# Five token groups instead of six in the input projection and the gates of a hybrid attention layer

## The chip, the cores and the metric

The kernel runs on one core of a Trainium2 chip. The metric is the device time of one execution in microseconds. The kernel before was timed three times: the median is 2660.56 us, the runs lie between 2659.95 and 2668.45 us.

## What is computed

One layer of a streaming encoder on 2176 tokens: 2048 of a new stream and 128 (8 streams of 16) that continue running streams with 2048 cached positions each. The model width is 1024. All arithmetic is float32. Cut to what matters:

```python
h    = rms_norm(x, g_in)
proj = einsum('btd,de->bte', h, w_in)
qa, ka, va, z_a, qd, ckv_in, kpe_in, z_b, m_a, m_b = split(proj)   # 512,512,512,512,512,256,64,512,1024,1024 columns
o_a  = diff_attention(rope(qa), rope(ka), va)       # 4 heads, chunk-causal mask
o_b  = mla_attention(q_lat, q_pe, ckv_rows, kpe_rows)  # 4 heads, chunk-causal mask
y_a  = (rms_norm(o_a, g_sub) * silu(z_a)) @ w_oa
y_b  = (o_b @ w_uv * silu(z_b)) @ w_ob
out  = x + (sigmoid(m_a) * y_a + sigmoid(m_b) * y_b) @ w_out
y    = rms_norm(out, g_final)
```

The rotated keys, the values, the compressed rows and the rotated positional keys are outputs too.

## The kernel before, in words

Float32 products are made of three passes: each operand is split into a high part in the type float32r and a low part (the rest), and the products high*high, low*high and high*low are added in PSUM (`_mm3`, lines 95 to 101). A product over the model width has eight row tiles of 128, so it is 24 matmuls, each with a new 128x128 weight and a moving tile as wide as the token group.

**Groups.** `GROUPS` (line 38) cuts the 2176 tokens into five groups of 384 and one of 256. All stages but the attention go by these groups.

**Phase A** (`_phase_a`, lines 127 to 347) is the input projection. `load_group` (151) loads a group of the transposed input in four staging tiles of two row tiles, writes the high and low parts `hi` and `lo` (they stay on chip until the phase ends) and sums the squares in a tile `sq`. `first_units` (271) does this while two units of 128 output columns are projected group by group; `stats` (184) makes the norm from the squares. A unit is one `unit_psum` per group (24 matmuls into one PSUM bank), and blocks of two units follow: `units`, `rope_block`, `kpe_block`, `v_block`. There are 14 units through `units` and `first_units` and 8 through the rope blocks; the key block has 16 matmuls per group, and the value blocks go by 128 tokens and don't depend on the groups. Each block's weights come through `weights` (201): a staging tile (`stage`, 141: of three one comes from the pool `a_s` with one buffer, the others from the outer pool `z_s` with two), a split on ACT and DVE, and a pair of buffers out of three pairs (`z_w` four buffers, `a_w` two). After blocks 2 to 9 the split weights of two gate units each are written to a scratch tensor `wz` (lines 342 to 347).

**Gates** (`_gates`, 350 to 389) are 16 more units of the same projection, done later as work that fills TensorE: the tile scheduler orders all instructions ahead of time by priority and by a model of their times, the gates' loads and splits have the priority of the end of phase A, their matmuls that of the code's place behind phase B. One group's `z_hi` and `z_lo` are on chip at a time (pool `z_h`, one buffer). Each unit has one PSUM bank (pool `z_p`, one buffer), which ACT empties with a tanh into a tile of `z_t` (4 buffers) that is stored to `smT`. Groups 0, 1, 3 and 4 load and split the weights anew, groups 2 and 5 load the split ones (`ready`). Groups 0, 1, 2 and 5 stand ahead of the sample part, 3 and 4 are tied behind the last attention matmul (lines 1276 to 1280).

**Phase A2** (`_phase_a2`) makes the latent queries, keys and values by groups. **Phase B** (`_phase_b`) is the attention of the 2048 tokens, four heads of each kind side by side: in eight steps the differential head goes up through the query blocks and the latent head goes down, so that at each step both together need 20 key and value tiles of 128x512. These tiles come from the pool `c_kv` with 25 buffers (line 925), loaded in the order of the code at line 943 and given to any buffer that has come free. At a change of heads 16 tiles of the new latent head and 4 of the new differential head take the place of the old ones. **The sample part** (`_sample`) reads the caches, and **phase C** (`_phase_c`) is the output side, by groups again. All DMAs of these parts are issued on SP's queue, in the order of the schedule.

Of the kernel before, what the change touches and what calls it, by code (L numbers as in the profile page):

```python
# [20 lines left out]
P = 128  # L21
# [15 lines left out]
NG = 384  # L37
GROUPS = [(t, min(NG, T - t)) for t in range(0, T, NG)]

# [76 lines left out]
def _outer(c, stack):  # L116

    tc = c.tc

    def pool(name, bufs, **kw):  # L120
        return stack.enter_context(tc.tile_pool(name=name, bufs=bufs, **kw))

    c.zh, c.zw, c.zs, c.zt = pool("z_h", 1), pool("z_w", 4), pool("z_s", 2), pool("z_t", 4)
    c.zp = pool("z_p", 1, space=PSUM)


def _phase_a(c):
    nc, tc = c.nc, c.tc
    with (
        tc.tile_pool(name="a_h", bufs=1) as ph,  # L130
        tc.tile_pool(name="a_w", bufs=2) as pw,
        tc.tile_pool(name="a_s", bufs=1) as pst,
        tc.tile_pool(name="a_t", bufs=6) as pt,
# [5 lines left out]
        count = {"st": 0, "w": 0, "t": 0}  # L139
# [11 lines left out]
        def load_group(g):  # L151
# [6 lines left out]
            for k2 in range(4):  # L158
# [62 lines left out]
        def rope_block(u0, dst, pair, out, scale):  # L221
            ws = [weights(c.i["wu"][u0 + i], f"u{u0 + i}") for i in range(2)]
            for g, (t0, n) in enumerate(GROUPS):
# [7 lines left out]
                ta, tb = tmp(n, f"ta{nm}"), tmp(n, f"tb{nm}")  # L231
# [160 lines left out]
def _phase_a2(c):  # L392
    nc, tc = c.nc, c.tc
    with (
# [20 lines left out]
        def tmp(n, name, m=P):  # L415
            return pt.tile([P, NG], F32, tag="t", name=name)[:m, :n]
# [11 lines left out]
        def prep(g):  # L428
            t0, n = GROUPS[g]
            qd = pn.tile([P, 4, NG], F32, tag="qd", name=f"qd{g}", bufs=1)[:, :, :n]  # L430
            nc.sync.dma_start(qd, c.qdT[:, :, t0 : t0 + n].rearrange("k p n -> p k n"))
            ck = pn.tile([P, 2, NG], F32, tag="ck", name=f"ck{g}", bufs=1)[:, :, :n]
            nc.sync.dma_start(ck, c.ckT[:, :, t0 : t0 + n].rearrange("k p n -> p k n"))
            sq = pn.tile([P, 4, NG], F32, tag="sq", name=f"sq{g}", bufs=1)[:, :, :n]
# [3 lines left out]
            sk = pn.tile([P, 2, NG], F32, tag="sk", name=f"sk{g}", bufs=1)[:, :, :n]  # L438
# [17 lines left out]
            for j, r in enumerate(rs):  # L456
# [5 lines left out]
                R = pn.tile([P, NG], F32, tag=f"R{j}", name=f"R{g}_{j}", bufs=1)[:, :n]  # L462
                nc.scalar.copy(R, pr[:, :n])
                Rs.append(R)
            qh = pn.tile([P, 4, NG], F32R, tag="qh", name=f"qh{g}")[:, :, :n]
            ql = pn.tile([P, 4, NG], F32R, tag="ql", name=f"ql{g}")[:, :, :n]
# [5 lines left out]
            ch = pn.tile([P, 2, NG], F32R, tag="ch", name=f"ch{g}")[:, :, :n]  # L472
            cl = pn.tile([P, 2, NG], F32R, tag="cl", name=f"cl{g}")[:, :, :n]
# [17 lines left out]
        def kpe(g):  # L491
            t0, n = GROUPS[g]
            cols = slice(t0, t0 + n)
            parts = pn.tile([64, 2, 2, NG], F32, tag="kp", name=f"kp{g}", bufs=1)[:, :, :, :n]
# [881 lines left out]
```

## Time and profile before

| | before |
|---|---|
| median of 3 runs | 2660.56 us |
| the profiled execution's own time | 2664.33 us |
| its span (first to last instruction) | 2662.4 us |
| mean granted TensorE clock | 0.975 |
| PE busy | 2521.9 us, 95% of the span |
| DVE / ACT / POOL busy | 54% / 40% / 26% |
| HBM traffic | 185 GB/s over the span |

A busy PE is read with care: the records of matmuls overlap, so that one of 334 ns can follow another after 173 ns. What a matmul costs in a steady stream is the distance of the starts. The granted clock stands as a share of 2.4 GHz; 0.50 is 1.2 GHz.

### The profile page before, as it was taken

What the parts mean: (1) busy time and instruction counts of PE and PEld (TensorE: products, weight loads), DVE (VectorE), ACT (ScalarE), POOL (GpSimd) and SP (SyncE); (2) the same over time, 40 slices, a digit from 0 to 9 for tenths busy, and PEclk for the clock granted to TensorE, in tenths of its full rate; (3) what the DMA queues carried; (4) which work ended last, traced back from release to release, by engine and by line L of the source; (5) the groups of instructions that cost most, each with busy time, mean ns of one, the idle gap of its engine ahead of it and who ended that gap; (6) DMA issues with size and microseconds to landing.
All of it is one profiled execution on the core that took longest, in us unless ns stands there. A gap on an engine that the chain in (4) does not pass through costs nothing. (4 is left out here: it accounts for less than half of the span.)

```text
span 2662.4 us, 44907 instructions
## 1 busy us (share of the span) xinstructions
PE 2521.9 (95%) x16308; PEld 2257.0 (85%) x16308; DVE 1438.3 (54%) x3038; ACT 1066.4 (40%) x2682; POOL 705.4 (26%) x946
## 2 busy tenths in 40 slices
PE   7999999999888989999999999998999998999998
PEld 7999999999787879998988898887676775888887
DVE  8236762233565657877785577896323323533334
ACT  5111213212334356766674566775334333311111
POOL 7102220001343433334343333544101001112212
PEclk9999999999898999999999999999999998999999
DMA  5345777422567893365566658523887676533332
GB/s 182 113 156 200 252 255 228 150 69 82 165 226 242 263 281 108 123 184 155 172 184 185 206 173 246 152 76 119 343 334 293 253 308 225 182 126 119 124 101 101
DMA packets 291372, 496.17 MB, mean 186 GB/s; under 512 B 27440, under 2 KB 229200, under 8 KB 280144
## 3 DMA queue, kind: packets, MB, share of 16 engines
q1 hardware_dynamic: 291152, 493.31, 55.9%
q8 instruction: 129, 2.11, 0.3%
q14 instruction: 91, 0.75, 0.1%
HBM read 351.55 MB, written 141.66 MB: 185 GB/s over the span
## 5 line engine op out<-in xcount | busy, mean ns | idle before, releaser
L98 PE MATMUL z<-z_hi,zw 128*128 128x384 f32 (+1 forms) x768 | 261.8, 341 | 21.9 <-ACT zt L388 18.5
L99 PE MATMUL z<-z_lo,zw 128*128 128x384 f32 (+1 forms) x768 | 257.1, 335 | 0.6 <-POOL z_lo L370 0.6
L100 PE MATMUL z<-z_hi,zw 128*128 128x384 f32 (+1 forms) x768 | 256.3, 334 | 0.4 <-DVE zw L113 0.2
L990 DVE TENSOR_REDUCE pmd<-sd 128x1 f32<-128x512 f32 (+3 forms) x320 | 189.3, 602 | 56.6 <-PE sd L1091 28.0
L992 ACT ACTIVATE ed<-sd,pmd 128x512 f32<-128x512 f32 (+3 forms) x320 | 200.7, 632 | 47.8 <-DVE pmd L990 32.2
L1091 PE MATMUL sd<-k,q 128*128 128x512 f32 (+2 forms) x640 | 190.2, 384 | 5.0 <-ACT ed L992 2.7
L1031 POOL TENSOR_SCALAR ed<-ed,ad 128x512 f32<-128x512 f32 (+3 forms) x160 | 115.6, 739 | 279.7 <-DVE ad L1007 129.4
L98 PEld LDWEIGHTS z<-z_hi,zw 128*128 128x128 f32 x768 | 147.2, 192 | 41.1 <-ACT zt L388 24.4
L99 PEld LDWEIGHTS z<-z_lo,zw 128*128 128x128 f32 x768 | 146.9, 191 | 8.9 <-issue 6.3
L100 PEld LDWEIGHTS z<-z_hi,zw 128*128 128x128 f32 x768 | 146.7, 191 | 6.7 <-issue 3.7
L1031 POOL TENSOR_SCALAR em<-em,am 128x512 f32<-128x512 f32 (+3 forms) x160 | 104.5, 669 | 154.3 <-DVE am L1007 108.9
L98 PE MATMUL y<-o,wh_ab 128*128 128x384 f32 (+1 forms) x384 | 129.5, 337 | 14.2 <-DVE sm L1210 12.5
L370 POOL TENSOR_TENSOR z_lo<-zx,z_hi 128x384 fp32r<-128x384 f32 (+1 forms) x48 | 48.5, 1038 | 329.6 <-DVE gt L260 261.6
L113 DVE TENSOR_TENSOR zw<-zs,zw 128x512 fp32r<-128x512 f32 x128 | 89.6, 727 | 82.4 <-ACT zw L112 82.1
L98 PE MATMUL ps_u<-hi,wh_u 128*128 128x384 f32 (+1 forms) x384 | 126.0, 328 | 6.1 <-ACT wh_u L112 6.1
L99 PE MATMUL y<-o,wh_ab 128*128 128x384 f32 (+1 forms) x384 | 128.0, 333 | 0.4 <-DVE o L113 0.4
L1215 ACT ACTIVATE m<-sm 128x384 fp32r<-128x384 f32 (+1 forms) x48 | 24.4, 507 | 258.6 <-POOL sm L1213 258.6
L100 PE MATMUL y<-o,wl_ab 128*128 128x384 f32 (+1 forms) x384 | 127.8, 333 | 0.0
L98 PE MATMUL ps_z<-hi,wh_z 128*128 128x384 f32 (+1 forms) x384 | 125.1, 326 | 1.0 <-ACT wh_z L112 1.0
L99 PE MATMUL ps_u<-lo,wh_u 128*128 128x384 f32 (+1 forms) x384 | 125.6, 327 | 0.0
L100 PE MATMUL ps_u<-hi,wl_u 128*128 128x384 f32 (+1 forms) x384 | 125.0, 327 | 0.0
L99 PE MATMUL ps_z<-lo,wh_z 128*128 128x384 f32 (+1 forms) x384 | 125.0, 325 | 0.0
(364 smaller groups left out, 7539.1 us busy)
## 6 DMA issues: line engine op xcount, KB each, us to landing
zs<-in_wu_dram SPq DMA_DIRECT2D x64, 512.0 KB
zw<-wz SPq DMA_DIRECT2D x64, 512.0 KB
ksd<-in_ckT_dram SPq DMA_DIRECT2D x32, 1024.0 KB
vsd<-in_cv_dram SPq DMA_DIRECT2D x32, 1024.0 KB
q<-Qs SPq DMA_DIRECT2D x128, 128.0 KB
ksm<-in_cc_dram SPq DMA_DIRECT2D x16, 1024.0 KB
smT<-zt SPq DMA_DIRECT2D x80, 192.0 KB
sm<-smT SPq DMA_DIRECT2D x80, 192.0 KB
```

What stands on the lines that cost most here:

```text
L98: nc.tensor.matmul(out, ah, bh, start=(j == 0), stop=False)
L99: nc.tensor.matmul(out, ah, bl, start=False, stop=False)
L100: last = nc.tensor.matmul(out, al, bh, start=False, stop=(j == n - 1))
L113: nc.vector.tensor_tensor(lo, src, hi.bitcast(F32), op=ALU.subtract)
L370: nc.gpsimd.tensor_tensor(lo[:, k], x[:, j], hi[:, k].bitcast(F32), op=ALU.subtract)
L990: nc.vector.tensor_reduce(nm_, ps[:, :w], axis=AX.X, op=ALU.max, negate=True)
L992: nc.scalar.activation(e[:, :w], ps[:, :w], AF.Exp, bias=nm_, accum_out=l[:, s, i : i + 1])
L1031: nc.gpsimd.tensor_scalar(p, p, a[:, 0, j : j + 1], 1.0, op0=ALU.mult, op1=ALU.mult)
L1091: nc.tensor.matmul(ps[:, :n], qs[s][:, j, qc], ks[s].tiles[i][:, :n], start=(j == 0), stop=(j == 1 and not last))
L1215: nc.scalar.mul(z[0], sm[0], 0.5)
```

## The change

Phase A and the gates go by five groups, two of 512 and three of 384 tokens (`GROUPS`); phases A2 and C keep the six old ones under the name `CGROUPS`. As the tiles of 512 need more room, other buffers go: the pool `a_s` (third staging buffer of phase A), one of four buffers of `z_t`, one of six of `a_t`, and four of 25 key and value buffers of `c_kv`. The sums of squares and two temporaries of the rope blocks move from `a_c` and `a_t` into `z_t` (`tmp2`). The gates are done for groups 0, 1 and 2 ahead of the sample part (before: 0, 1, 2 and 5), only group 2 with weights that are split already.

```diff
-NG = 384
-GROUPS = [(t, min(NG, T - t)) for t in range(0, T, NG)]
+NG = 512
+GROUPS = [(0, 512), (512, 512), (1024, 384), (1408, 384), (1792, 384)]
+NC = 384
+CGROUPS = [(t, min(NC, T - t)) for t in range(0, T, NC)]
...
-    c.zh, c.zw, c.zs, c.zt = pool("z_h", 1), pool("z_w", 4), pool("z_s", 2), pool("z_t", 4)
+    c.zh, c.zw, c.zs, c.zt = pool("z_h", 1), pool("z_w", 4), pool("z_s", 2), pool("z_t", 3)
...
-        tc.tile_pool(name="a_s", bufs=1) as pst,
-        tc.tile_pool(name="a_t", bufs=6) as pt,
+        tc.tile_pool(name="a_t", bufs=5) as pt,
...
         def stage(shape, name):
-            count["st"] += 1
-            return (pst if count["st"] % 3 == 0 else c.zs).tile(shape, F32, tag="st", name=name)
+            return c.zs.tile(shape, F32, tag="st", name=name)
...
-                        total = pc.tile([P, NG], F32, tag="sq", name=f"sq{g}", bufs=2)[:, :n]
+                        total = tmp2(n, f"sq{g}")
...
-                ta, tb = tmp(n, f"ta{nm}"), tmp(n, f"tb{nm}")
+                ta, tb = tmp2(n, f"ta{nm}"), tmp2(n, f"tb{nm}")
...
-        tc.tile_pool(name="c_kv", bufs=25, reuse_waits="tile") as pkv,
+        tc.tile_pool(name="c_kv", bufs=21, reuse_waits="tile") as pkv,
...
-            for g in (0, 1, 2, 5):
-                _gates(c, prio, g, None, g in (2, 5))
+            for g in (0, 1, 2):
+                _gates(c, prio, g, None, g == 2)
```

The lines left out put `CGROUPS` and `NC` for `GROUPS` and `NG` in phases A2 and C and change nothing else there.

## Rows read from the trace of the kernel before

**Rows 1.** The page, busy time of PE: engine, us, share, instructions.

```profile
PE 2521.9 (95%) x16308; PEld 2257.0 (85%) x16308; DVE 1438.3 (54%) x3038; ACT 1066.4 (40%) x2682; POOL 705.4 (26%) x946
```

**Rows 2.** Windows: us, busy us of PE, PEld, DVE, ACT, POOL; PEclk, DMA share, GB/s.

```profile
0.00:70.00 70.00, 53.39 (x268) 51.07 (x269) 59.47 (x87) 38.14 (x75) 51.83 (x65) 0.93 0.58 185
70.00:655.00 585.00, 572.24 (x3675) 571.16 (x3674) 245.42 (x394) 116.42 (x204) 63.47 (x60) 0.99 0.50 166
...
690.00:938.00 248.00, 208.88 (x1119) 198.16 (x1118) 150.70 (x242) 97.27 (x191) 100.24 (x94) 0.90 0.76 240
...
1391.00:1641.00 250.00, 240.70 (x1628) 215.62 (x1627) 165.24 (x425) 144.78 (x416) 87.25 (x137) 0.98 0.65 202
1641.00:1850.00 209.00, 197.10 (x1305) 168.37 (x1305) 170.30 (x447) 143.69 (x415) 93.78 (x142) 0.98 0.38 112
```

**Rows 3.** PE's timeline, width 384, first and last of 97: start us, us.

```profile
99.80 0.33 PE L99 MATMUL ps_qd<-lo,wh_qd 128*128 128x384 f32 x1
...
116.44 0.33 PE L99 MATMUL ps_qd<-lo,wh_qd 128*128 128x384 f32 x1
```

**Rows 4.** PE's timeline, width 256: first of 48, and what follows them.

```profile
540.65 0.28 PE L98 MATMUL ps_z<-hi,wh_z 128*128 128x256 f32 x1
...
546.40 0.34 PE L98 MATMUL ps_z<-hi,wh_z 128*128 128x384 f32 x1
```

**Rows 5.** PE's timeline in phase C, width 512: first and last of seven.

```profile
2272.91 0.39 PE L1224 MATMUL out<-wl_o,m 128*128 128x512 f32 x1
...
2274.27 0.39 PE L1224 MATMUL out<-wl_o,m 128*128 128x512 f32 x1
```

**Rows 6.** The page, the costliest group: xcount, busy us, mean ns, idle before.

```profile
L98 PE MATMUL z<-z_hi,zw 128*128 128x384 f32 (+1 forms) x768 | 261.8, 341 | 21.9 <-ACT zt L388 18.5
```

**Rows 7.** PE's waits: who waited for whom, us in total, times, longest.

```profile
PE z L98 <- ACT zt L388: 18.5, 15, 2.4
...
PE ps_qd L98 <- ACT hi L170: 7.9, 1, 7.9
...
PE ps_u L98 <- ACT wh_u L112: 6.1, 3, 4.1
PE psr L197 <- DVE dg L196: 6.0, 4, 2.6
PE sm L1130 <- DMA kn<-Kn: 5.6, 2, 4.8
...
PE psv L99 <- DVE wl_v L113: 3.0, 1, 3.0
...
PE pss L189 <- POOL sq L181: 2.6, 1, 2.6
...
PE ps_qd L99 <- DVE lo L171: 2.3, 1, 2.3
...
PE z L98 <- ACT z_hi L369: 2.1, 1, 2.1
```

**Rows 8.** SP's timeline, key loads at three changes of heads: start us, us.

```profile
1191.89 1.34 SPq L943 DMA_DIRECT2D kn<-Kn  x2
...
1194.77 3.07 SPq L943 DMA_DIRECT2D k<-Ks  x2
...
1418.02 0.38 SPq L943 DMA_DIRECT2D kn<-Kn  x1
...
1422.04 6.14 SPq L943 DMA_DIRECT2D k<-Ks  x2
...
1655.73 1.63 SPq L943 DMA_DIRECT2D kn<-Kn  x2
...
1659.58 6.51 SPq L943 DMA_DIRECT2D k<-Ks  x2
```

**Rows 9.** PE's timeline behind the change to the third heads.

```profile
1419.57 1.11 PE L1130 MATMUL sm<-kn,qn 128*128 128x384 f32 x2 [4.76 <-DMA kn<-Kn]
```

**Rows 10.** Windows, the six microseconds from there.

```profile
1419.00:1425.00 6.00, 5.43 (x14) 4.36 (x15) 1.13 (x3) 0.37 (x1) 0.00 (x0) 0.50 0.91 249
```

More of the change, by code (lines that the diff above doesn't have):

```diff
@@ L138, in _phase_a @@
         R = pc.tile([P, T], F32, name="R")
-        count = {"st": 0, "w": 0, "t": 0}
+        count = {"w": 0}
         def stage(shape, name):
-            count["st"] += 1
-            return (pst if count["st"] % 3 == 0 else c.zs).tile(shape, F32, tag="st", name=name)
+            return c.zs.tile(shape, F32, tag="st", name=name)
         def tmp(n, name, m=P):
@@ L415, in tmp @@
         def tmp(n, name, m=P):
-            return pt.tile([P, NG], F32, tag="t", name=name)[:m, :n]
+            return pt.tile([P, NC], F32, tag="t", name=name)[:m, :n]
         def pair(n, name):
@@ L437, in prep @@
             nc.vector.tensor_tensor(sq[:, 0], sq[:, 0], sq[:, 1], op=ALU.add)
-            sk = pn.tile([P, 2, NG], F32, tag="sk", name=f"sk{g}", bufs=1)[:, :, :n]
+            sk = pn.tile([P, 2, NC], F32, tag="sk", name=f"sk{g}", bufs=1)[:, :, :n]
             nc.scalar.square(sk, ck)
@@ L471, in prep @@
                 nc.gpsimd.tensor_tensor(ql[:, kt], x, qh[:, kt].bitcast(F32), op=ALU.subtract)
-            ch = pn.tile([P, 2, NG], F32R, tag="ch", name=f"ch{g}")[:, :, :n]
-            cl = pn.tile([P, 2, NG], F32R, tag="cl", name=f"cl{g}")[:, :, :n]
+            ch = pn.tile([P, 2, NC], F32R, tag="ch", name=f"ch{g}")[:, :, :n]
+            cl = pn.tile([P, 2, NC], F32R, tag="cl", name=f"cl{g}")[:, :, :n]
             for kt in range(2):
@@ L491, in kpe @@
         def kpe(g):
-            t0, n = GROUPS[g]
+            t0, n = CGROUPS[g]
             cols = slice(t0, t0 + n)
-            parts = pn.tile([64, 2, 2, NG], F32, tag="kp", name=f"kp{g}", bufs=1)[:, :, :, :n]
+            parts = pn.tile([64, 2, 2, NC], F32, tag="kp", name=f"kp{g}", bufs=1)[:, :, :, :n]
             src = c.kpT.rearrange("(l r) t -> r l t", l=2)[:, :, cols]
@@ L500, in kpe @@
             nc.gpsimd.tensor_tensor(x, x, parts[:, 1], op=ALU.add)
-            cs = pn.tile([64, 2, NG], F32, tag="kcs", name=f"kcs{g}", bufs=1)[:, :, :n]
+            cs = pn.tile([64, 2, NC], F32, tag="kcs", name=f"kcs{g}", bufs=1)[:, :, :n]
             nc.sync.dma_start(cs, c.i["ropek"][:, :, cols])
@@ L511, in group @@
         def group(g, qh, ql, ch, cl):
-            t0, n = GROUPS[g]
+            t0, n = CGROUPS[g]
             cols = slice(t0, t0 + n)
@@ L527, in group @@
             pa, pb = pab
-            cs = pn.tile([P, 2, NG], F32, tag="cs", name=f"cs{g}", bufs=1)[:, :, :n]
+            cs = pn.tile([P, 2, NC], F32, tag="cs", name=f"cs{g}", bufs=1)[:, :, :n]
             nc.sync.dma_start(cs, c.i["rope"][:, :, cols])
@@ L565, in _phase_a2 @@
         next(ahead)
-        for g in range(len(GROUPS)):
+        for g in range(len(CGROUPS)):
             work = group(g, *next(ahead))
-            if g + 1 < len(GROUPS):
+            if g + 1 < len(CGROUPS):
                 kpe(g)
@@ L1180, in tmp @@
         def tmp(n, name):
-            return pt.tile([P, NG], F32, tag="t", name=name)[:, :n]
+            return pt.tile([P, NC], F32, tag="t", name=name)[:, :n]
         def load_o(t0, n):
@@ L1186, in load_o @@
             for half in range(2):
-                x = po.tile([P, 4, NG], F32, tag="x", name=f"ox{t0}_{half}")[:, :, :n]
+                x = po.tile([P, 4, NC], F32, tag="x", name=f"ox{t0}_{half}")[:, :, :n]
                 nc.sync.dma_start(x, c.oT[4 * half : 4 * half + 4, :, t0 : t0 + n].rearrange("k p n -> p k n"))
@@ L1191, in load_o @@
                     if half == 0:
-                        r = pt.tile([P, NG], F32, tag="r", name=f"r{t0}_{k}", bufs=2)[:, :m]
+                        r = pt.tile([P, NC], F32, tag="r", name=f"r{t0}_{k}", bufs=2)[:, :m]
                         nc.sync.dma_start(r, c.rsub[k, t0 : t0 + m].partition_broadcast(P))
                         nc.gpsimd.tensor_tensor(x[:, j, :m], x[:, j, :m], r, op=ALU.mult)
-                    z = [po.tile([P, NG], F32R, tag=f"o{l}{k}", name=f"o{l}{k}_{t0}")[:, :n] for l in range(2)]
+                    z = [po.tile([P, NC], F32R, tag=f"o{l}{k}", name=f"o{l}{k}_{t0}")[:, :n] for l in range(2)]
                     _split(nc, z[0], z[1], x[:, j])
@@ L1213, in merge @@
             nc.gpsimd.tensor_tensor(sm[0], sm[0], sm[1], op=ALU.add)
-            z = [(pv if u < 2 else pm).tile([P, NG], F32R, tag=f"m{l}{u}", name=f"m{l}_{nm}")[:, :n] for l in range(2)]
+            z = [(pv if u < 2 else pm).tile([P, NC], F32R, tag=f"m{l}{u}", name=f"m{l}_{nm}")[:, :n] for l in range(2)]
             nc.scalar.mul(z[0], sm[0], 0.5)
@@ L1225, in project @@
                 nc.tensor.matmul(ps[i], m[1][:, ts], a[:, hs], start=False, stop=(u == 7))
-        for t0, n in GROUPS:
+        for t0, n in CGROUPS:
             o = load_o(t0, n)
```

14 lines of the change are left out of this document (7 added, 7 removed).

## The prediction, made before the changed kernel was built or run

> **What bounds the kernel now.** I read the page first: PE is busy for 95% of the span, the other engines for 54% and less [rows 1], so the first question is what a matmul costs and how many are left. Then the windows by stage, to see where PE is not the bound: in the first 70 us it is busy for 53.4 us at a granted clock of 0.93 while DVE is busy for 59.5 (the loading and splitting of the input leads); from 70 to 655 us it is busy for 572 of 585 us at 0.99 (the projection is PE's); from 690 to 938 us (phase A2) for 209 of 248 at 0.90; in the later heads of the attention for 241 of 250 and 197 of 209 [rows 2]. Last PE's waits, for the places where the buffers that the change takes away already bind [rows 7].
>
> **What a matmul costs.** In a steady stream 96 steps of width 384 take 116.44 - 99.80 = 16.64 us, 173.3 ns each [rows 3]; 48 of width 256 take 5.75 us, 119.8 ns each [rows 4]; six of width 512 take 1.36 us, 226.7 ns each [rows 5]. From 256 to 384 that is 0.418 ns per column, one column per cycle at 2.4 GHz, and from 384 to 512 the same (53.4 ns). What is left is fixed: 119.8 - 256 x 0.418 = about 13 ns per matmul, whatever its width. The change keeps all columns and drops matmuls, so this is what it can save.
>
> The Trainium skill (TensorE: Matmul & The Clock Gate, section "Wait — 56ns, not 53.3ns?") puts the fixed cost of a matmul in a steady stream at about 2.5 ns over its columns; by that the whole change would save 928 x 2.5 = 2.3 us, an estimate from that page. The rows above disagree, and the measurement decides.
>
> **Part 1, the matmuls.** Per row tile and pass, six matmuls (five of 384, one of 256) become five (two of 512, three of 384): 2 x 173.3 + 119.8 - 2 x 226.7 = 13.0 ns less. A unit has 24 of these, 0.312 us. There are 22 units in the projection and 16 in the gates (768 matmuls per pass, 16 x 8 x 6 [rows 6]), 38 in all: 11.9 us; the key block's 16 add 0.2. Sum: 928 matmuls and **-12.1 us**, 7.1 of it in the projection, where PE is the bound, and 5.0 in the gates. The gates fill PE in phases A2 and B; as PE is nearly full there, less filling work lets the attention end earlier, so I count it whole. Ends: 12.1 if all of it shows, 7.1 if the gates' part falls into idle time.
>
> **Part 2, the gates' single PSUM bank.** PE waits 18.5 us in 15 waits for ACT to empty it [rows 7]. 80 units instead of 96 empty it 16 times less: 18.5 x 16/96 = 3.1 us at most, nothing if the waits that remain are the same ones. I take **-2**. One change of the gates' group less (0 to 1 to 2, then the sample part) can save the 2.1 us wait for z_hi [rows 7], or nothing: **-1**. The gates also issue 32 loads of split weights and 16 stores of smT less on SP; SP is never what PE waits for by itself, so I cost that at nothing. DVE and ACT split weights for two groups out of three there as for two out of four before: no more work.
>
> **Part 3, the start.** The first group is a third wider, so the first waits grow: 7.9 us for hi, 2.3 for lo, 2.6 for the squares [rows 7]. All of hi, lo and squares together are the same columns in fewer instructions, and DVE is the leader there, so the loading as a whole ends a little sooner. But the last group is 384 instead of 256 wide, and what PE must do after the last load grows by 48 matmuls of 128 more columns, 48 x 0.0535 = 2.6 us. The sums of squares now share three buffers of z_t with the results on their way to memory: the first square of a group can wait for a store, and behind it on ACT stand the group's hi parts, for which PE waits; the nearest row is the 6.0 us of four waits for the norm [rows 7]. Ends: -3 (loading shorter by that much) and +6; I take **+1**.
>
> **Part 4, one staging buffer less in phase A.** At a change of blocks PE waits today 6.1 us in three waits and 3.0 in one for split weights [rows 7]; those wait for weight buffers, not for staging. With two staging buffers, those hold the weights that wait for a buffer at the end of a block, and the load of the next ones starts only when one of them has been split. A second unit is needed one group later than the first (24 x 226.7 ns = 5.4 us), which covers a load; only the value blocks need both weights at once. Ends: 0, and once more 4.1 + 3.0 = 7 us; I take **+2**, nearer the covered end. The rope blocks have eight temporaries where they had six, and DVE waits less, not PE: nothing. The value blocks' z tiles drop to three buffers; what PE waits for in that block today is the weights alone [rows 7], as six more PSUM banks are ahead: nothing.
>
> **Part 5, the key buffers.** Within a head 20 of the tiles are in use at every step, so 25 buffers leave five to load ahead and 21 leave one. The loads go in a fixed order, each into the next buffer that is released. With four fewer, each load gets the release that today's load four places later gets. At the three changes of heads the last key tile of the new latent head is issued by 1193.23, 1418.40 and 1657.36 us, and the load four places later (the second of the k pair) by 1197.84, 1428.18 and 1666.09: later by 4.6, 9.8 and 8.7 us, 23.1 in all [rows 8]. Already today PE stood still for 4.76 us at the second of these changes [rows 9], and then ran at a granted clock of 0.50 for the next six microseconds [rows 10], which cost 3 us more. So the ends are 0, if gate matmuls and the older heads' products fill PE, and 23.1 + 3 x 3 = 32 us. What speaks for the low end is that gates are still there to fill at all three changes, and that the order is planned with these releases known; in the last head they run out. I take **+5**, about one more wait like that of today.
>
> **Sum.** -12.1 - 2 - 1 + 1 + 2 + 5 = -7.1 us. The profiled execution took 2664.33 us (span 2662.4), 3.8 above the median of the runs; the difference is set against the median: 2660.56 - 7.1 = **2653.5 us**. What this kernel's measurement can tell from no change is about 0.3%, 8 us.
>
> **The rivals.**
> *The keys bind.* PE stands at each change of heads because the last key chunk can be loaded only when the old head's product has released its values. For it: the wait of 4.76 us exists with five spare buffers [rows 9]. Against: filling work. Price: 32 instead of 5, so 2653.5 + 27 = 2680 us. It makes the kernel slower by more than 8 us from the point where the keys cost over 20 us (-15.1 + 3 + 20 = +8). Chance 0.20, spread over 2669 to 2690.
> *All of it is covered.* No new wait in staging and keys, and the start gains its 3 us: -15.1 - 3 = -18, 2642.5 us. For it: the waits today are few against 2660 us. Chance 0.20.
> *Start and staging eat the gain.* Parts 3 and 4 at their upper ends, +6 and +7: -15.1 + 13 + 5 = +3, 2663.5 us. For it: DVE leads the first 70 us, and the two staging buffers are now shared by input and weights. Chance 0.06.
> *The change saves hardly any time on PE*: the 13 ns belong to something other than the count of matmuls and stay: -7.1 + 12.1 = +5.0, 2665.5 us. The three widths on one line [rows 3 to 5] speak against it. Chance 0.02. By the rule of the Trainium skill told above (TensorE: Matmul & The Clock Gate) it would come out so, 2.3 us lower.
>
> **How the numbers follow.** The forecast has 0.52, with its own range 2646 to 2661; its centre is 0.9 us short of the bound of 8 us, so a little under half of it (0.25) counts as faster and 0.27 as the same. Faster: 0.25 + 0.20 = 0.45. Same: 0.27 + 0.06 + 0.02 = 0.35. Slower: 0.20. The range leaves out the lower half of the covered case and the upper half of the keys' case, 0.10 each: 2643 to 2676 us.
>
> **What would show it.** In the profile after: PE instructions fewer by 928 (a few more or less for lost records); 512-wide matmuls of ps_u and z 227 ns apart; the stretch from the first load to the end of phase A shorter by about 4 us (7.1 less parts 3 and 4); z waits for zt of about 15 to 16 us; PE waits for kn, k or v at changes of heads of some 10 us in all, against 5.6 for kn today [rows 7]. The forecast is wrong if the attention from 938 to 1850 us grows by more than 15 us (the keys), or if the first 655 us don't get shorter (start and staging).

## The result, and the profile after

The changed kernel takes 2680.19 us (median of 6 runs, 2673.34 to 2681.70) against 2661.97 us of the kernel before in the same session (6 runs, 2654.62 to 2668.45): 1.0064 times as long, 95% interval 1.0045 to 1.0082. It is slower by about 17 us, where I had forecast 7 us less. The profiled execution after took 2673.34 us, the lowest of its runs, while that of before lay 3.8 us above the median of its three runs; the two spans, 2671.4 and 2662.4 us, are therefore closer together than the medians.

The page of the changed kernel, busy time of PE and the gates' group:

```profile
PE 2510.5 (94%) x15380; PEld 2157.1 (81%) x15380; DVE 1431.1 (54%) x2963; ACT 1056.7 (40%) x2629; POOL 701.4 (26%) x920
...
L100 PE MATMUL z<-z_hi,zw 128*128 128x384 f32 (+1 forms) x640 | 241.7, 378 | 35.2 <-ACT zt L388 33.7
```

Against [rows 1] there are 16308 - 15380 = 928 matmuls fewer, as counted, and PE is busy for 11.4 us less. So the work did leave PE, and the time did not follow. PE's timeline of the changed kernel, 59 matmuls of width 512 in a row in phase A, the first and the last (start us, us):

```profile
288.72 0.39 PE L100 MATMUL ps_u<-hi,wh_u 128*128 128x512 f32 x1
...
301.87 0.39 PE L100 MATMUL ps_u<-hi,wh_u 128*128 128x512 f32 x1
```

58 steps in 13.15 us are 226.7 ns each, what [rows 5] said of width 512.

Windows by stage of the changed kernel (columns as in [rows 2]):

```profile
0.00:70.00 70.00, 49.98 (x225) 43.50 (x226) 50.96 (x68) 33.46 (x57) 45.31 (x53) 0.93 0.53 170
70.00:655.00 585.00, 572.79 (x3231) 530.69 (x3230) 240.66 (x353) 116.69 (x197) 71.43 (x53) 0.99 0.51 170
690.00:938.00 248.00, 205.62 (x1046) 183.76 (x1044) 150.94 (x231) 92.58 (x178) 95.27 (x90) 0.90 0.72 224
1391.00:1641.00 250.00, 235.00 (x1476) 201.95 (x1474) 177.11 (x451) 153.91 (x432) 98.45 (x148) 0.98 0.55 169
1641.00:1850.00 209.00, 196.25 (x1292) 164.21 (x1291) 174.82 (x464) 146.79 (x427) 88.34 (x136) 0.98 0.35 100
```

In three of these windows PE is busy for several us less than in [rows 2]: for 50.0 us of the first 70 where it was 53.4, for 205.6 from 690 to 938 us where it was 208.9, and for 235.0 from 1391 to 1641 us where it was 240.7. The waits of PE in the changed kernel (who waited for whom, us in total, times, longest) point to the first of them at once and say little of the last:

```profile
PE z L100 <- ACT zt L388: 33.7, 18, 6.5
...
PE ps_qd L100 <- ACT hi L170: 11.7, 1, 11.7
...
PE psr L197 <- DVE dg L196: 6.5, 4, 3.7
...
PE sm L1130 <- DMA kn<-Kn: 4.5, 3, 2.3
PE pss L189 <- POOL sq L181: 3.2, 1, 3.2
...
PE ps_u L100 <- ACT wh_u L114: 2.9, 3, 1.0
```

The first matmul waits 11.7 us for its input instead of 7.9 [rows 7]; the wait for `lo` behind it is shorter, 1.2 us instead of 2.3. The wait for key tiles `kn`, where I had looked for the loss, is shorter than before: 4.5 us instead of 5.6. Phase A ends at 681.7 us, where it was 688.6.

**Where the time went.** The last value product of phase A2 marks the time at which the attention can start; from there to the last attention product it takes 920.0 us before and 924.5 after. That looks like little, but the work in it is not the same, since gates fill it. The gates' matmuls in the trace of the kernel before, in the windows from that last value product to the first differential product, and then head by head (us, PE busy, granted clock, DMA share, GB/s):

```profile
926.30:942.90 16.60, 12.39 (x65) 0.97 0.86 261
942.90:1170.90 228.00, 77.52 (x378) 0.99 0.53 163
1170.90:1391.00 220.10, 61.59 (x289) 1.00 0.57 172
1391.00:1641.00 250.00, 79.90 (x474) 0.98 0.65 202
1641.00:1846.30 205.30, 9.39 (x60) 0.98 0.37 108
```

And in the changed kernel:

```profile
930.50:955.50 25.00, 16.77 (x65) 0.93 1.00 305
955.50:1189.00 233.50, 85.11 (x316) 0.99 0.47 143
1189.00:1419.80 230.80, 73.61 (x298) 1.00 0.53 163
1419.80:1653.80 234.00, 46.95 (x226) 0.98 0.54 161
1653.80:1855.00 201.20, 0.17 (x2) 0.98 0.33 95
```

The gates are used sooner: by PE's busy time more of them ahead of the attention and in the first two heads, 226 matmuls instead of 474 in the third head, none in the last. More of them went into phase A2 too. From the end of phase A to the last value product, PE on gates, first before, then the changed kernel (us, PE busy, granted clock, DMA share, GB/s):

```profile
688.60:926.30 237.70, 56.82 (x272) 0.90 0.76 240
```

```profile
681.70:930.50 248.80, 67.61 (x248) 0.90 0.72 225
```

Phase A2 is 11.1 us longer, and PE is busy with gates for 10.8 us more of it. The last gate ahead of the sample part ends at 1541.8 us instead of 1670.2. Counted at their steady steps of 119.8, 173.3 and 226.7 ns the gates in this stretch are 198.7 us of work before and 184.7 after. The stretch less its gates, the number by which the kernels are compared below, is 920.0 - 198.7 = **721.3 us** before and 924.5 - 184.7 = **739.8 us** after: 18.5 us longer with the gates taken out. The two spans lie only 9.0 us apart, as phase A, 6.9 us shorter in this profile, and the 5 us of gates saved pull the other way.

### The profile page after: what moved, and what is told of

Same layout as the page of the kernel before. It is cut to its first block, busy times and chain, and to the rows that moved or that the text cites. A ratio compares the mean times of both kernels' runs of the same rounds, so it can differ in the third digit from the quotient of the medians.

```text
span 2671.4 us, 42648 instructions
## 1 busy us (share of the span) xinstructions
PE 2510.5 (94%) x15380; PEld 2157.1 (81%) x15380; DVE 1431.1 (54%) x2963; ACT 1056.7 (40%) x2629; POOL 701.4 (26%) x920
## 5 line engine op out<-in xcount | busy, mean ns | idle before, releaser
L100 PE MATMUL z<-z_hi,zw 128*128 128x384 f32 (+1 forms) x640 | 241.7, 378 | 35.2 <-ACT zt L388 33.7
L102 PE MATMUL z<-z_hi,zw 128*128 128x384 f32 (+1 forms) x640 | 235.5, 368 | 0.6 <-DVE zw L115 0.6
L101 PE MATMUL z<-z_lo,zw 128*128 128x384 f32 (+1 forms) x640 | 236.0, 369 | 0.0
L100 PEld LDWEIGHTS z<-z_hi,zw 128*128 128x128 f32 x640 | 123.4, 193 | 63.9 <-ACT zt L388 41.1
L102 PEld LDWEIGHTS z<-z_hi,zw 128*128 128x128 f32 x640 | 123.0, 192 | 17.1 <-issue 5.0
L101 PEld LDWEIGHTS z<-z_lo,zw 128*128 128x128 f32 x640 | 123.5, 193 | 15.1 <-issue 5.0
L992 ACT ACTIVATE em<-sm,pmm 128x512 f32<-128x512 f32 (+3 forms) x160 | 100.0, 627 | 70.3 <-DVE pmm L990 64.3
L1091 PEld LDWEIGHTS sd<-k,q 128*128 128x128 f32 x640 | 105.3, 192 | 26.0 <-ACT ed L992 11.9
L1213 POOL TENSOR_TENSOR sm<-sm,sm 128x384 f32<-128x384 f32 (+1 forms) x48 | 51.9, 1082 | 254.0 <-DVE sm L1210 254.0
L990 DVE TENSOR_REDUCE pmm<-sm 128x1 f32<-128x512 f32 (+3 forms) x160 | 96.2, 604 | 40.6 <-PE sm L1134 26.9
L100 PE MATMUL ps_u<-hi,wh_u 128*128 128x384 f32 (+1 forms) x320 | 114.9, 359 | 2.9 <-ACT wh_u L114 2.9
```

The costliest lines, as they stand in the source:

```text
L100: nc.tensor.matmul(out, ah, bh, start=(j == 0), stop=False)
L101: nc.tensor.matmul(out, ah, bl, start=False, stop=False)
L102: last = nc.tensor.matmul(out, al, bh, start=False, stop=(j == n - 1))
L990: nc.vector.tensor_reduce(nm_, ps[:, :w], axis=AX.X, op=ALU.max, negate=True)
L992: nc.scalar.activation(e[:, :w], ps[:, :w], AF.Exp, bias=nm_, accum_out=l[:, s, i : i + 1])
L1091: nc.tensor.matmul(ps[:, :n], qs[s][:, j, qc], ks[s].tiles[i][:, :n], start=(j == 0), stop=(j == 1 and not last))
```

## The experiments

The change has four parts that can be made alone: the groups of phase A, the groups of the gates, the small buffers of phase A (third staging buffer; temporaries), and the key buffers. The theories at stake are those of the prediction: the keys bind, the start and the staging bind, or neither does and the loss lies elsewhere. The table has what was timed, and two readings of each trace: the end of phase A, and the attention stretch less its gates, as defined above. Each ratio is against the kernel before timed in the same session, whose median lay between 2659.85 and 2663.61 us; the differences in us below are worked out from the ratios.

| run | keys | third staging | groups A / gates | median us, ratio [95%] | A ends | stretch less gates |
|---|---|---|---|---|---|---|
| before | 25 | yes | 6 / 6 | | 688.6 | 721.3 |
| changed | 21 | no | 5 / 5 | 2680.19, 1.0064 [1.0045, 1.0082] | 681.7 | 739.8 |
| e1 | 21 | yes | 6 / 6 | 2680.34, 1.0071 [1.0046, 1.0096] | 682.2 | 738.3 |
| e7 | 21, padded | yes | 6 / 6 | 2678.67, 1.0083 [1.0056, 1.0109] | 686.4 | 742.2 |
| e8 | 23 | yes | 6 / 6 | 2666.83, 1.0019 [1.0002, 1.0036] | 684.3 | 726.0 |
| e2 | 25 | no | 6 / 6 | 2677.84, 1.0058 [1.0037, 1.0079] | 693.3 | 722.9 |
| e5 | 25 | no | 6 / 6 | 2669.72, 1.0043 [1.0026, 1.0059] | 696.6 | 722.7 |
| e6 | 25 | yes | 6 / 6 | 2660.90, 1.0005 [0.9988, 1.0021] | 681.1 | 724.3 |
| e3 | 25 | yes | 5 / 6 | 2654.61, 0.9974 [0.9956, 0.9991] | 675.8 | 718.5 |
| e10 | 25 | yes | 5 / 6 | 2654.44, 0.9968 [0.9952, 0.9984] | 673.0 | 722.5 |
| e9 | 21 | no | 6 / 6 | 2686.09, 1.0092 [1.0063, 1.0121] | 691.6 | 738.1 |
| e13 | 21 | no | 5 / 6 | 2677.64, 1.0059 [1.0042, 1.0075] | 685.1 | 735.3 |
| e4 | 21 | no | 6 / 5 | 2695.65, 1.0117 [1.0085, 1.0150] | 694.1 | 743.4 |
| e12 | 21 | yes | 5 / 5 | 2674.21, 1.0042 [1.0027, 1.0057] | 678.5 | 737.9 |

(Of the runs e1 to e13 all but e1, e5, e7 and e8 also have the change's fewer temporaries.)

### The key buffers: e1, e7, e8

e1 is the kernel before with one number changed:

```diff
-        tc.tile_pool(name="c_kv", bufs=25, reuse_waits="tile") as pkv,
+        tc.tile_pool(name="c_kv", bufs=21, reuse_waits="tile") as pkv,
```

> The kernel before with one edit: 21 key and value buffers instead of 25; the groups, the staging and the computation stay. Keys theory (late keys hold the attention back at the changes of heads, so the gates' filling work is used up sooner and the end of the attention stands uncovered): 10 to 20 us slower than before, about 2675 us, the gates ahead of the sample part done earlier than at 1690 us. Gates theory (the wider gate units and their order in phases A2 and B cost the time, not the keys): within 4 us of before. Staging theory: no difference either.

It is 1.0071 times as slow as before, about 19 us: the keys alone cost as much as the whole change. e7 adds a tile of 8 KB per partition that nobody reads, so that all later tiles keep their addresses:

```diff
+        tc.tile_pool(name="c_pad", bufs=1, reuse_waits="tile") as ppad,
...
+        pad = ppad.tile([P, 2048], F32, name="pad")
+        nc.gpsimd.memset(pad[:, 0:1], 0.0)
```

> 21 key and value buffers as in e1, but with 8 KB left unused behind them, so that the tiles allocated after them (kp, the queries) lie at the same addresses as before; one memset of one column is added. If the number of buffers is what costs (late keys): as e1, 12 to 20 us slower than before, the gates done by 1630 us. If it is where the later tiles lie (kp and the queries over tiles of phase A2 that come free late, so the attention starts later): within 4 us of before, the first score matmul 16 to 18 us after the last of phase A2.

1.0083, about 22 us, and the first differential product comes 29.0 us after the last of phase A2 (26.9 in e1, 16.6 before): it is the number of buffers, not where the other tiles lie. e8 has `bufs=23`:

> The kernel before with 23 key buffers instead of 25 (three to load ahead in place of five; 21 leave one). Theory (each buffer taken away makes every load wait for a later release, and the plan answers in proportion): about half of what 21 cost (17 to 19 us), so 2667 to 2673 us, 1.002 to 1.0045 of before. Rival (only the last buffers count, since a step of the heads changes two or three tiles and three spare ones are still enough for that): no loss, 2658 to 2664 us, 0.999 to 1.001. In its profile the theory wants the first differential products of heads 1 and 2 some 5 to 10 us later than with 25 buffers, measured from the start of the attention; the rival wants them unmoved.

1.0019, about 5 us with an interval from 0.5 to 10: nearer a quarter than half of what 21 cost, though half lies at the edge of the interval. The stretch, 726.0 us, lies between those of 21 and 25 keys and nearer to 25. Neither of the two readings expected was quite right, and that the last two spare buffers carry most of the price is likely, not shown.

The stretches of all the kernels of the table fall apart by the keys alone: 718.5 to 724.3 us in the six with 25 keys, 735.3 to 743.4 in the seven with 21.

In e1 the stretch is 17 us longer (738.3 - 721.3), though PE's waits for `kn` come to 6.6 us at line 1130, where they were 5.6. The gates' matmuls of e1, same windows and columns as above:

```profile
923.70:950.60 26.90, 22.00 (x113) 0.95 1.02 310
950.60:1171.80 221.20, 70.23 (x337) 0.99 0.48 146
1171.80:1410.40 238.60, 76.80 (x355) 0.99 0.57 177
1410.40:1660.80 250.40, 76.84 (x463) 0.97 0.67 205
1660.80:1860.80 200.00, 0.16 (x1) 0.98 0.31 90
```

Before the first differential product PE does 113 gate matmuls where it did 65, and in the second head 355 where it did 289. I read this as gates being run where steps of the attention stood, as fewer tiles are loaded ahead. They don't cover all of it. All engines in the second head, first before, then e1 (columns as in [rows 2]):

```profile
1170.90:1391.00 220.10, 218.88 (x1428) 195.02 (x1428) 168.11 (x430) 142.96 (x409) 91.16 (x149) 1.00 0.57 172
```

```profile
1171.80:1410.40 238.60, 231.63 (x1490) 205.87 (x1489) 171.48 (x442) 148.04 (x418) 89.52 (x150) 0.99 0.57 177
```

The head is 18.5 us longer, and PE stands still for 7.0 us of it instead of 1.2, in two waits above all:

```profile
PE sm L1130 <- DMA kn<-Kn: 3.3, 1, 3.3
PE sm L1130 <- ACT ed L992: 2.9, 1, 2.9
```

The gates end at 1629.8 us instead of 1670.2, and the third change of heads finds none. All engines in the 100 us from 40 us ahead of the first product of the last head, first before, then e1, then the changed kernel (columns as in [rows 2]):

```profile
1601.00:1701.00 100.00, 96.34 (x663) 84.88 (x662) 78.87 (x189) 65.86 (x188) 47.20 (x67) 0.98 0.76 228
```

```profile
1620.80:1720.80 100.00, 87.44 (x545) 73.72 (x544) 76.00 (x194) 66.65 (x192) 46.76 (x69) 0.93 0.55 163
```

```profile
1613.80:1713.80 100.00, 89.84 (x545) 72.63 (x544) 77.18 (x200) 66.44 (x199) 43.62 (x68) 0.95 0.49 141
```

PE stands still for 3.7, 12.6 and 10.2 us of the 100, and the granted clock falls from 0.98 to 0.93 and 0.95. e1's waits of PE in that window are spread over the attention's own chain, `kn` being only one of them:

```profile
PE ptd L1045 <- DVE ptld L1049: 3.4, 2, 2.2
PE sm L1130 <- DMA kn<-Kn: 3.0, 1, 3.0
PE sd L1091 <- ACT em L992: 2.4, 2, 2.3
PE od L1105 <- DVE ogd L1104: 1.6, 1, 1.6
```

### Small buffers of phase A: e2, e5, e6

All three have six groups and 25 keys. e5 takes the third staging buffer away and nothing else:

```diff
-        tc.tile_pool(name="a_s", bufs=1) as pst,
-            return (pst if count["st"] % 3 == 0 else c.zs).tile(shape, F32, tag="st", name=name)
+            return c.zs.tile(shape, F32, tag="st", name=name)
```

e6 keeps it and takes the temporaries away as the change does; e2 has both edits:

```diff
-    c.zh, c.zw, c.zs, c.zt = pool("z_h", 1), pool("z_w", 4), pool("z_s", 2), pool("z_t", 4)
+    c.zh, c.zw, c.zs, c.zt = pool("z_h", 1), pool("z_w", 4), pool("z_s", 2), pool("z_t", 3)
-        tc.tile_pool(name="a_t", bufs=6) as pt,
+        tc.tile_pool(name="a_t", bufs=5) as pt,
-                        total = pc.tile([P, NG], F32, tag="sq", name=f"sq{g}", bufs=2)[:, :n]
+                        total = tmp2(n, f"sq{g}")
-                ta, tb = tmp(n, f"ta{nm}"), tmp(n, f"tb{nm}")
+                ta, tb = tmp2(n, f"ta{nm}"), tmp2(n, f"tb{nm}")
```

> The kernel before with its six groups and 25 key buffers, but with the change's smaller buffers of phase A: no third staging buffer, z_t with three buffers, a_t with five, the sums of squares and the rope temporaries in z_t. Staging theory: 8 us or more slower, and phase A ends later than at 688.6 us. Keys theory and gates theory: within 4 us of before, and phase A ends at 686 to 693 us.

> The kernel before without the third staging buffer of phase A, and nothing else. If the staging buffer is what made e2 slower: the first matmul at about 11 us instead of 7.9 (the first input tile waits until the first weights have left their staging buffer), phase A ends 5 us or more later, 8 to 15 us slower in all. If it was the smaller temporaries of e2: within 4 us of before, the first matmul at 8 us.

> The kernel before with the temporaries moved as in the change (sums of squares and two rope temporaries in z_t, which has three buffers instead of four, and five instead of six a_t), the third staging buffer, six groups and 25 keys kept. Theory (the temporaries hide; the loss of the small buffers comes from staging and keys): 2658 to 2665 us, 0.9985 to 1.0015 of before. Rival (the gates wait for a z_t tile that is stored late, and the sums of squares for a store): 2667 to 2672 us, 1.002 to 1.004, with more waits of z for zt in its profile than the 18.5 us of before.

e6 costs nothing (1.0005), e5 1.0043 (11 us) and e2 1.0058 (15 us): the loss is the staging buffer's. The waits of PE in e5 up to 697 us show where it is in that trace:

```profile
PE ps_qd L98 <- ACT hi L168: 11.3, 1, 11.3
PE ps_u L98 <- ACT wh_u L112: 8.9, 3, 6.3
...
PE ps_u L100 <- DVE wl_u L113: 3.3, 1, 3.3
...
PE ps_z L98 <- ACT wh_z L112: 2.5, 2, 1.5
PE ps_qd L99 <- DVE lo L169: 0.8, 1, 0.8
```

One more line of the kernel before, which [rows 7] leave out, is a wait for split weights:

```profile
PE ps_z L98 <- ACT wh_z L112: 1.0, 1, 1.0
```

The first wait is 3.4 us longer than in [rows 7], and the wait for `lo` behind it 1.5 us shorter. The waits for split weights come to 8.9 + 3.3 + 2.5 us and 0.9 on two smaller lines, 15.6 us, where before has 6.1 + 3.0 + 1.0 = 10.1. (In e2, which has two staging buffers as well, they are 11.4 us, so this part varies.) ACT's timeline in e5 tells why the first is longer:

```profile
10.66 0.61 ACT L168 ACTIVATE hi<-xt,vec 128x384 fp32r<-128x384 f32 x1 [1.75 <-DMA xt<-in_xT_dram]
11.18 0.51 ACT L175 ACTIVATE sq<-xt 128x384 f32<-128x384 f32 x1
```

Line 175 (177 in the kernel before) is the square of the first row tile alone. That tile is converted last of the early ones, at 10.66 us, since its load has to wait for a staging buffer: both hold `ws_qd`, the first weights, until those have been split.

### Five groups in phase A alone: e3, e10

`AGROUPS` stands in phase A's loops, `GROUPS` (six) everywhere else; the third staging buffer and 25 keys stay. e3:

```diff
+NA = 512
+AGROUPS = [(0, 384), (384, 512), (896, 512), (1408, 384), (1792, 384)]
```

e10 has the wide groups last:

```diff
-AGROUPS = [(0, 384), (384, 512), (896, 512), (1408, 384), (1792, 384)]
+AGROUPS = [(0, 384), (384, 384), (768, 384), (1152, 512), (1664, 512)]
```

> Five groups in phase A alone (384, 512, 512, 384, 384, so that the first group's tiles stay at 384), the gates with their six groups, 25 key buffers and the third staging buffer kept, z_t with three buffers of 512. All theories: phase A ends about 7 us earlier than before (681 to 683 us). Keys theory and gates theory: that gain stays, 2653 to 2657 us. If the later phases lose it again although neither the keys nor the gates changed, the plan of the order is at fault: 2660 us or more.

> As e3 (five groups in phase A alone, 25 keys, third staging buffer), with the wide groups last: 384, 384, 384, 512, 512. If the width of the first loads matters in the first 70 us, this is up to 4 us faster than e3 (2650 us); if the wider last group keeps PE longer behind the last load, 2 to 3 us slower (2657 us); if only the number of matmuls counts, the same, 2653 to 2656 us.

Both are faster than before, 0.9974 and 0.9968, 7 and 8.5 us, and no other kernel here is: the matmuls left out of phase A are real time. (e3's phase A ended at 675.8 us, earlier than the 681 to 683 that I expected.) The order of the widths makes no difference that these runs can tell.

The ends of phase A in all traces agree with this, taken as four cells. Six groups with the third staging buffer end it at 681.1 to 688.7 us (mean of seven 684.9), without it at 691.6 to 696.6 (mean of four 693.9); five groups with it at 673.0 to 678.5 (three, 675.8), without it at 681.7 to 685.1 (three, 683.2; the kernels of the table and of the last group of runs below). Five groups are worth 9 to 11 us by these means, the buffer 7.4 to 9.

### All buffers, and one set of groups at a time: e9, e4, e13

e9 has all the change's smaller pools and six groups throughout; e4 has them with five groups in the gates alone, e13 with five groups in phase A alone.

> All the smaller buffers of the change (21 keys, two staging buffers, z_t and a_t and what moves into them) with the six old groups: the change without its groups. If the parts add up: 17 (e1) + 14 (e2) = 31 us slower than before, about 2694 us, and the changed kernel is then 14 us faster than this one, which is what the five groups give back. If the groups give nothing: about 2680 us, as the changed kernel.

> Six groups in phase A, five in the gates, 21 key buffers, two staging buffers. Phase A as before (688 us, or up to 4 later by the staging). Keys theory: as e1 less the 5 us of the gates' matmuls, 2665 to 2675 us. Gates theory: as the changed kernel plus the 7 us that phase A then lacks, about 2685 us, while e1 is like before.

> The changed kernel with the gates in the six old groups again (0, 1, 2 and 5 ahead of the sample part); phase A in the same five groups, all the small buffers as in the change. Theory (the gates are filler, and 5 us less of it ahead of the end of the attention only leave PE without work there): as fast as the changed kernel or a little faster, 2668 to 2680 us, 1.002 to 1.007 of before, with gates until 1630 to 1670 us instead of 1541. Rival (the 384 matmuls less of the gates show in the time with 5 us or more, as I predicted): 2684 to 2688 us, 1.0085 to 1.010.

From e9 (1.0092) to e13 (1.0059) the groups of phase A give 9 us back, as in e3. From e13 to the changed kernel (1.0059 to 1.0064) and from e9 to e4 (1.0092 to 1.0117) the gates' five groups give nothing that these runs can tell, though they are 384 matmuls fewer. The traces of e13 and the changed kernel show the exchange: the stretch is 9.6 us shorter (924.5 us for 934.1), and phase A2, with more gates in it, 9.4 us longer (248.8 for 239.4). e4 lies above both times that I had expected of it; its 7 us over e9 are within the two intervals. e9 is 24.5 us above before, less than the 15 of e2 and the 19 of e1 added up; with intervals of 6 to 8 us to either side these may still add, and that is left open. The mirror image of e3, five groups in the gates with 25 keys, was not run.

### The third staging buffer in the changed kernel: e12

The changed kernel with `a_s` put back, and four `a_t` buffers instead of five to make room.

> The changed kernel with the third staging buffer of phase A put back (one a_t buffer goes for the room). Theory (the third buffer is worth 8 to 10 us also with wide groups, as the first load no longer waits): 2669 to 2674 us, 1.003 to 1.0045 of before, the first matmul at 8 us instead of 11.7 and phase A over by 672 to 676 us instead of 681.7. Rival (wide groups give each load more time, so that two buffers are enough behind the start, and the start comes back later): 2677 to 2681 us, 1.006 to 1.0075, phase A over by 678 to 682 us.

1.0042, 6 us less than the changed kernel: the ratio is at the upper edge of what the first theory asked. Phase A ends at 678.5 us, which is the rival's range (678 to 682), 3.2 us ahead of the changed kernel's. The first matmul starts at 8.5 us, as the theory had it:

```profile
8.52 1.22 PE L100 MATMUL ps_qd<-hi,wh_qd 128*128 128x512 f32 x2 [8.52 <-ACT hi L172]
```

So of the 11.7 us of the changed kernel 3.2 are the staging buffer's and 0.6 the wider group's. With the wait for `lo` the start is 10.9 us in e12 and 12.9 in the changed kernel, and the waits for split weights are 5.1 and 8.4 us.

### Are the gates used up, or are the keys late? e14, e15, e16

These cross the two. e14 has 25 keys and fewer gates ahead, as group 5 goes behind the attention:

```diff
-            for g in (0, 1, 2, 5):
-                _gates(c, prio, g, None, g in (2, 5))
+            for g in (0, 1, 2):
+                _gates(c, prio, g, None, g == 2)
...
-            for g in (3, 4):
+            for g in (5, 3, 4):
```

e15 is e1 (21 keys) with more gates ahead:

```diff
-            for g in (0, 1, 2, 5):
-                _gates(c, prio, g, None, g in (2, 5))
+            for g in (0, 1, 2, 5, 3):
+                _gates(c, prio, g, None, g in (2, 5, 3))
...
-            for g in (3, 4):
+            for g in (4,):
```

e16 is the changed kernel with the same:

```diff
-            for g in (0, 1, 2):
-                _gates(c, prio, g, None, g == 2)
+            for g in (0, 1, 2, 3):
+                _gates(c, prio, g, None, g in (2, 3))
...
-            for g in (3, 4):
+            for g in (4,):
```

> The kernel before (25 key buffers, all else kept) with the gates of group 5 moved behind the last attention matmul, so that 46 us less of gates stand ahead and they run out by about 1560 to 1600 us instead of 1670. Theory 'gates run out' (the stops around the third change of heads are there because nothing is left to fill them): PE stands still for 8 us or more in the 100 us from 40 us ahead of the first product of the last head (3.7 us in the kernel before) and gets fewer than 600 matmuls done there (663 before). Rival 'late keys' (the stops belong to the 21 buffers): 5 us of standing still or less there, with 25 buffers. In the time either theory allows 2652 to 2672 us, as the gates of group 5 fill gaps of the sample part in exchange.

> The kernel before with 21 key buffers and the gates of group 3 moved ahead of the sample part (with split weights loaded), so that 66 us more of gates stand ahead and last until about the end of the attention. Theory 'gates run out': PE stands still for 5 us or less in the 100 us around the third change (12.6 us with 21 keys and the old gates), and the stretch from the first differential product to the end of the attention, less its work, gets 8 us or more back; if the sample part has gaps left by the missing gates, they take some of it again, 2662 to 2678 us in all. Rival 'late keys': 9 us or more of standing still there though gates are left, 2678 to 2690 us.

> The changed kernel with the gates of group 3 ahead of the sample part too (four groups ahead, one behind; group 3 with split weights loaded). Theory 'gates run out': PE stands still for 5 us or less around the third change instead of 10.2, and the time falls by 3 to 10 us against the changed kernel, to 2668 to 2676 us (1.002 to 1.005 of before), less what the sample part loses. Rival 'late keys': no less standing still around the third change, and 2677 to 2688 us, since the sample part has 66 us less of gates to fill its gaps.

| | keys | gates ahead end, us | gates in the stretch, us | stretch less gates, us | still at the third change, us | ratio [95%] |
|---|---|---|---|---|---|---|
| before | 25 | 1670.2 | 198.7 | 721.3 | 3.7 | |
| e14 | 25 | 1482.3 | 152.7 | 738.0 | 7.4 | 1.0220 [1.0179, 1.0261] |
| e1 | 21 | 1629.8 | 198.8 | 738.3 | 12.6 | 1.0071 [1.0046, 1.0096] |
| e15 | 21 | 1892.8 | 265.3 | 720.9 | 2.9 | 1.0151 [1.0107, 1.0194] |
| changed | 21 | 1541.8 | 184.7 | 739.8 | 10.2 | 1.0064 [1.0045, 1.0082] |
| e16 | 21 | 1762.7 | 251.2 | 718.9 | 0.6 | 1.0063 [1.0035, 1.0091] |

The same 100 us in e14, e15 and e16:

```profile
1567.90:1667.90 100.00, 92.60 (x569) 75.17 (x570) 81.40 (x214) 70.63 (x211) 44.70 (x70) 0.97 0.50 144
```

```profile
1628.60:1728.60 100.00, 97.09 (x604) 86.14 (x604) 67.87 (x168) 60.20 (x167) 41.94 (x63) 0.97 0.74 231
```

```profile
1635.60:1735.60 100.00, 99.36 (x613) 88.03 (x612) 65.92 (x160) 58.30 (x165) 36.91 (x59) 1.00 0.72 218
```

The stretch less its gates grows by 17 us with 25 keys when gates are taken from it, and gets 17 to 21 back with 21 keys when they are given to it. As time, e14's stretch is 29 us shorter for 46 us of gates taken, and e15's 49 us longer than e1's for 67 given: part of the gates runs in time that is bare without them. (e14's 7.4 us of standing still fall short of the 8 that I had asked, but its 569 matmuls in the window are under 600 where before has 663.) Head by head, each from its first differential product to that of the next, the stretch less its gates (us):

| | up to the first differential product | head 1 | head 2 | head 3 | head 4 |
|---|---|---|---|---|---|
| before | 5.5 | 162.5 | 170.0 | 185.3 | 198.1 |
| e1 | 7.5 | 162.9 | 177.2 | 190.9 | 199.8 |
| changed | 10.5 | 161.8 | 171.7 | 194.8 | 201.0 |
| e14 | 9.3 | 164.4 | 170.9 | 196.9 | 196.4 |
| e15 | 7.4 | 162.6 | 177.2 | 183.0 | 190.7 |
| e16 | 10.5 | 161.8 | 170.3 | 176.3 | 199.9 |

In the changed kernel the last two heads have 12.4 of the 18.5 us. There the gates that run out are the larger cause: the third head is 11.6 us longer than before's in e14, with 25 keys and gates until 1482 us, and in e16, with 21 keys and gates until 1763 us, it is 18.5 us shorter than the changed kernel's. In e1 it is otherwise: 9.6 of its 17 us come ahead of the third head, while gates are left, and the 7.2 of the second head stay in e15 with all its gates. Gates that run out can't be the cause of these; the waits in that head, 3.3 us for `kn` in e1 and 3.9 in e15, point to the late keys themselves. e15's total hides them because its last two heads, filled to the end, are 9.7 us shorter than those of before. What 25 keys with e15's gates would give was not run, so how much the keys cost where gates never run out is open for the last two heads.

The times that the first theory gave for these three were too low, by 44 us in e14, 19 in e15 and 2 in e16, as I had priced the gates' other use too low. e16's time lies in the range of the rival, but its 0.6 us of standing still doesn't fit it. In e16 the stretch gives 20.9 us and the sample part takes them back. The windows of the sample part, first of the changed kernel, then of e16:

```profile
1855.00:2265.70 410.70, 390.92 (x3354) 280.31 (x3354) 133.87 (x300) 145.15 (x377) 52.82 (x85) 0.99 0.78 298
```

```profile
1900.70:2273.90 373.20, 341.42 (x2969) 231.32 (x2969) 108.23 (x260) 119.56 (x321) 43.88 (x77) 0.92 0.76 293
```

With 66.4 us of gates fewer it is only 37.5 us shorter, so 28.9 us are lost: PE stands still for 31.8 us of it instead of 19.8, and the granted clock is 0.92 instead of 0.99. In e14 the gates that went behind last until 2269 us, beyond the last sample product at 2209, and the first product of phase C comes at 2279 us (before: gates until 2205, that product at 2217). The gates are one budget: in each of these three kernels something stands bare in the place that they were taken from.

## Why the prediction was wrong

**Part 1 was right for the projection and wrong for the gates.** The 13 ns per matmul hold. Phase A, priced at -7.1 us, gave 7 and 8.5 us in e3 and e10, with intervals of 4 to 5 us to either side. The Trainium skill (TensorE: Matmul & The Clock Gate, section "Wait — 56ns, not 53.3ns?") would give the 544 matmuls of phase A 2.5 ns each, 1.4 us, an estimate from that page; the traces don't agree, and the steps of 226.7 ns above are again 13 ns over their columns. The gates, -5.0 us, gave nothing (e13 against the changed kernel). The step that failed is "as PE is nearly full there, less filling work lets the attention end earlier, so I count it whole". PE is not full by itself there but by the gates; with fewer of them, and more of those run in phase A2, the end of the attention is bare for longer. The lower end that I gave, the 7.1 alone, was the right value.

**Part 2** went the other way: PE's wait for `zt` rose from 18.5 to 33.7 us, with one wait of 6.5 (e13 and e9, with six groups in the gates, have 34.0 and 32.1, so it isn't the groups). In sum it need not cost time: e3 has 28.9 us of it and is faster than before. But one wait, of 4.9 us, stands ahead of the changed kernel's first differential product, where its stretch loses 5.0 (table by heads); whether that one costs time is open. PE's waits from 930.5 to 955.5 us, the longest:

```profile
PE z L100 <- ACT zt L388: 4.9, 1, 4.9
```

The wait for `z_hi`, priced at -1, is no longer to be seen.

**Part 3** (+1) holds by the first product of e12, 8.5 us against 7.9; no run takes the wider first group apart from the rest of it.

**Part 4** (+2 in 0 to 7) was 6 us in e12's comparison and 11 in e5, by the ends of phase A 7.4 to 9. The step that failed is that I let the staging buffers hold weights only "at the end of a block". At the start both hold the first weights while the first row tile of the input waits for one; and at the changes of blocks the waits for split weights grew by 5.5 us in e5 and by 3.3 from e12 to the changed kernel, which my cover of one group's matmuls was to hide.

**Part 5** (+5 in 0 to 32) is where the prediction fell: the term put at 5 measured 19 us alone in e1, 22 in e7. The bounds held and the choice between them didn't. I went to the low end because "gates are still there to fill at all three changes", which holds in the kernel before, where they last until 1670 us. But a late key is covered by running a gate sooner, and each gate run sooner is missing later. The cover I named was being spent by the very thing it covered; I named no work for the time after. And it was not whole while it lasted: the second head of e1 loses 7.2 us with gates at hand. The rival "the keys bind" had 2680 us, the time measured, but by luck: its price of 32 us was too high by 10 to 13, about what the gates' 5.0 us and the staging's 5 were wrong the other way, and PE's waits for `kn` at the changes of heads, which it names, come to 5.4 us in the changed kernel.

The sum with measured terms: -9 (phase A) + 0 (gates) + 1 (start) + 7 (staging) + 18 (attention stretch) = +17, as timed. The terms come from different runs, none known better than to some 4 us, so that it meets the time to the microsecond is luck too.

**The signs I named** were partly wrong too. The matmul count and the step of 227 ns came as said. Phase A ended 6.9 us earlier in the two profiles, where I had said 4; by the means of the four cells above it is 1.7. The waits of `z` for `zt` were to be 15 to 16 us and were 33.7, those for keys some 10 us and were 5.4 (4.5 and 0.9 on two lines). And I had said that the keys would show as attention growing by more than 15 us: from the first differential product to its end it takes 903.4 us before and 899.5 after. It got shorter because gates had moved out of it; only the stretch less its gates shows the 18.5 us.

**The version that beats both** is e10 (2654.44 us) or e3 (2654.61): five groups in phase A alone, with six in the gates, the third staging buffer and all 25 key buffers kept.

## What to carry to other kernels

Work that fills gaps is a budget: before you cost an edit at nothing because filling work covers it, find in the trace where that work ends, and what stands bare if it ends sooner. A late load covered by filling work shows in the waits only in part (3.3 us for `kn` in the second head of e1, of 7.2 lost there); compare stretches at equal work, by taking the filling work out of them. And when buffers are taken away to pay for a wider tile, price the first load of the program as well as the steady state.

## What was not expected of the hardware

With the same order of PE's units phase A ended at 681.1 to 688.7 us in seven profiles, a spread of 7.6 us, as large as what was to be measured; the times of many runs, not one profile's stage, decide at this size. The granted clock went with it: 0.93 over the first 70 us in the three that ended at 686.4 us or later, 0.95 in the other four. A spare key buffer may have no fixed price: the first two that went cost 5 us (e8), the next two 14 more (e1), with intervals of some 5 us (e8) and 7 us (e1) to either side. And PE's granted clock was lower where PE stood still for longer: in the 100 us around the third change of heads it was 0.93 in e1, with 12.6 us of standing still, 0.95 in the changed kernel with 10.2, 0.97 or 0.98 in three kernels with 2.9 to 7.4, and 1.00 in e16 with 0.6.
